# A hybrid encoder layer on one core: all merge gates in the hyena stage, hyena's half of the merge ahead of the last softmax, joint weights spread by transposes

## The chip, the cores and the metric

The kernel runs on one core of a Trainium2 chip. The metric is device time in microseconds of one execution, launch to end; a run's time is given beside the span of its profile, which reaches from the first to the last instruction. A core has TensorE (PE; matmuls and transposes, with its weight loads shown as PEld), VectorE (DVE), ScalarE (ACT), GpSimd (POOL) and SyncE (SP), which issues nearly all of this kernel's DMAs in one queue, in program order.

## The reference

One layer with sequence length 1024 and model width 1024, all in float32. From `h`, a modulated layer norm of `x`, one projection feeds two branches, two silu gates and 2048 merge gates:

```python
h = (_layer_norm(x) * (1.0 + scale) + shift).astype(x.dtype)
p = h @ w_in + b_in
p_qkv, g_attn, p_hy, g_hy, r_merge = jnp.split(p, [i1, i2, i3, i4], axis=-1)
r_attn, r_hy = jnp.split(r_merge, 2, axis=-1)
...
    o_g, lse_g = dilated_window_attention(qkv[:, :, 0, g], qkv[:, :, 1, g], qkv[:, :, 2, g],
                                          slopes, dilation, radius)
...
wts = jax.nn.softmax(jnp.stack(lses, axis=0), axis=0)
o_attn = jnp.einsum('gbsh,gbshe->bshe', wts.astype(x.dtype), jnp.stack(outs, axis=0))
y_attn = o_attn.reshape(B, S, D_ATTN) * jax.nn.silu(g_attn)
...
for o, gate_o in enumerate((x1, x2)):
    z = gate_o * (bidirectional_long_conv(z, filters[:, o, 0], filters[:, o, 1]) + filt_bias[o] * z)
y_hy = z * jax.nn.silu(g_hy)

merged = jax.nn.sigmoid(r_attn) * (y_attn @ w_proj_attn) + jax.nn.sigmoid(r_hy) * (y_hy @ w_proj_hyena)
out = merged @ w_out + b_out
res = DEEPNORM_ALPHA * x.astype(jnp.float32) + (gate * out).astype(jnp.float32)
return (_layer_norm(res) * ln_g + ln_b).astype(x.dtype)
```

There are eight heads of 64 in three groups (window, dilation): (128, 1), (512, 4), (2048, 16). The joint weights `wts` say, per head and position, how much each group's output counts.

## The kernel before

Channels lie on the 128 partitions and positions along the free axis, so a product's output is a tile of 128 channels by 512 positions. Each matrix product is done in three passes: every operand is split into a high and a low part of reduced precision (fp32r), and high x high, high x low and low x high are summed in one PSUM tile. So every weight slice costs a ScalarE cast (`wh`, L222) and a GpSimd subtraction (`wl`, L223), and `h` itself is kept as two resident tiles `hTh` and `hTl` of 128 x 8 x 1024. The function `proj` makes one slice of 128 output channels as two products of 24 matmuls of 512 columns (L242).

The stages in program order:
- norm, filters and hyena (to about 640 us): four long convolutions, each a chain of transforms whose short products (`z`, `q`, `px`) alternate with VectorE and ScalarE work (`f`, `yh`, `yl`). They stand in `conv_order`, at a high priority of the scheduler; other products fill in between them.
- attention (640 to 1258 us), four pairs of heads, some 146 us each: `qkv` projections, the first softmax with one group, `values_pi` for the other two groups' values, `silu_out` (the silu gate of the pair's output), the second softmax with two groups (`softmax_av`, L906 to L934, tiles `ss`, `sx`, `pp`, `pt`, `po`), and the joint weights (L1022 to L1058). The last use of `h` in a pair is `silu_out`.
- merge and output (1258 us to the end): for each half of the positions, eight slices, each with a product of 12 matmuls with the hyena output and one of 12 with the attention output, each multiplied by its gate; their sum is split and goes into the output product with `w_out` (24 matmuls a group, L1138), followed by the residual, the last norm and the stores.

A merge gate is one slice of `proj` with a tanh, stored to `r_d` in DRAM: `gate_r`. There are sixteen, 0 to 7 for attention and 8 to 15 for hyena. `fill(n)` places the next n of the early ones; `N_EARLY` (12) says how many are early, `GATES` and `FILLS` how many stand behind each filter and each convolution. With 12 early, the last entry of `FILLS` finds none left. Gates 12 to 15 stand in a loop after attention:

```python
for j in range(N_EARLY, 16):
    gate_r(j, lambda: at.tile([P, 1152], F32, name="thr", tag="tmp")[:, 0:512])
hctx.close()
```

The joint weights `f` of a pair (2 orders x 8 blocks x 2 heads for 128 positions) have to be spread over the 64 channels of each head. Before, one transpose makes 32 rows of them (`pp` to `fr`, L1039), these go to DRAM (`wt_d`), and four DMA loads bring them back repeated over 64 partitions (`wt`). VectorE multiplies both parts with them, adds, multiplies with the silu gate and stores `ho` to `ya_d` (L1052 to L1058).

The merge loop (L1074 to L1109) loads the halves of `yh_d` and `ya_d` and splits them, then for each slice loads both weights into one tile `wr`, splits it, loads two gates `thr`, and does the two products `pj` (L1103), the gating (L1104), the sum (L1105) and the split into `mh`, `ml` (L1107, L1108). In the first half `w_out` is loaded behind it (L1121), eight tiles of 128 x 1024 through two buffers `wor`, each split by ScalarE (`woh`, L1122) and VectorE (`wol`, L1123).

The order of the instructions is made by a scheduler that walks the program with priorities; memory comes from pools, in which a tile of a tag waits for the release of an older one (`bufs`), and a pool opened where another was closed waits for that one's last readers. Within an engine, and within SyncE's queue, everything runs strictly in the order so made.

## Time and profile before

| | |
|---|---|
| time, median of 3 runs | 1461.62 us (1458.76 to 1461.76) |
| the profiled execution, its time | 1466.4 us |
| its span | 1464.6 us |
| TensorE busy | 1351.3 us, 92% of the span |
| VectorE, ScalarE, GpSimd busy | 65%, 43%, 19% |
| mean granted clock of TensorE | 0.970 |

Times are microseconds unless marked ns. Busy shares are means over the whole span; a window shows the same for a stretch of it, with the granted TensorE clock (1.00 is its full speed) and the share of the DMA engines' time. The chain of waits is followed back from the last instruction, at each step to what released it. In a timeline, what stands in brackets is the idle time before an instruction and what ended it.

### The profile page before, as it was taken

To read this page: it belongs to the slowest core of one execution; us is meant where nothing else is said; L and a number is where in the kernel's file an instruction comes from. 1 tells how busy PE (TensorE), PEld (TensorE's weight loads), DVE (VectorE), ACT (ScalarE), POOL (GpSimd) and SP (SyncE) were. 2 spreads that over 40 slices of the span, in tenths; PEclk is the share of its full clock that TensorE was granted. 3 is DMA by queue.
4 is the path that set the end of the run, shared out by engine and by line. 5 is a ranking of instruction groups with operands and counts; after the bars stand their busy time and mean duration, and the time that the engine had idled before them with its cause. 6 is when DMAs were issued, how large, how long until landed. Compare 5 with 4: busy or idle time off the path is not lost.

```text
span 1464.6 us, 18389 instructions
## 1 busy us (share of the span) xinstructions
PE 1351.3 (92%) x6707; PEld 1098.4 (75%) x6707; DVE 957.6 (65%) x1709; ACT 624.4 (43%) x1220; POOL 282.2 (19%) x160
## 2 busy tenths in 40 slices
PE   4788979889899999999999999999999999689997
PEld 1467767767777777788988788878887888567886
DVE  4798768767999898745156714761466144288866
ACT  1544444534244443446355534663466343242110
POOL 1221121210113122141121112111211111231220
PEclk9799999999999999999999999999999999899999
DMA  9633544332112222121113421311131114588523
GB/s 255 182 97 105 175 133 149 110 130 79 54 58 69 87 65 79 58 84 30 44 59 116 103 61 58 92 30 43 59 91 31 44 58 123 184 249 220 158 88 72
DMA packets 157024, 145.86 MB, mean 100 GB/s; under 512 B 16611, under 2 KB 126591, under 8 KB 156678
## 3 DMA queue, kind: packets, MB, share of 16 engines
q1 hardware_dynamic: 156486, 140.44, 32.7%
q0 software_dynamic: 288, 4.19, 0.8%
q8 instruction: 53, 0.87, 0.3%
q14 instruction: 37, 0.30, 0.1%
q10 hardware_dynamic: 160, 0.06, 0.0%
HBM read 116.73 MB, written 27.92 MB: 99 GB/s over the span
## 4 chain that ended last, share of the span: by engine, by line
PE 64%; DVE 11%; DMA 5%; ACT 3%; issue 2%; POOL 1%; SPq 0%; DVEq 0%; ACTq 0%; POOLq 0%
PE pj L242 33%; PE pj L888 6%; PE z L521 6%; PE po L1138 6%; PE pj L1103 4%; PE po L929 2%; PE pp L922 2%; DVE iv L447 2%; DVE f L447 1%; DMA dk<-in_t_dec 1%; DMA wor<-in_w_out 1%; PE z L531 1%; PE ss L859 1%; DVE f L459 1%; DVE q L447 1%
## 5 line engine op out<-in xcount | busy, mean ns | idle before, releaser
L223 POOL TENSOR_TENSOR wl<-wr,wh 128x1024 fp32r<-128x1024 f32 x88 | 234.8, 2668 | 966.9 <-ACT wh L222 895.7
L242 PE MATMUL pj<-hTh,wh 128*128 128x512 f32 x1024 | 407.5, 398 | 4.0 <-ACT hTh L433 4.0
L242 PE MATMUL pj<-hTl,wh 128*128 128x512 f32 x1024 | 407.1, 398 | 1.5 <-POOL hTl L435 0.8
L242 PE MATMUL pj<-hTh,wl 128*128 128x512 f32 x1024 | 408.1, 399 | 0.0
L242 PEld LDWEIGHTS pj<-hTl,wh 128*128 128x128 f32 x1024 | 194.3, 190 | 40.5 <-DVE hTl L435 2.2
L242 PEld LDWEIGHTS pj<-hTh,wh 128*128 128x128 f32 x1024 | 194.4, 190 | 39.9 <-ACT hTh L433 4.1
L242 PEld LDWEIGHTS pj<-hTh,wl 128*128 128x128 f32 x1024 | 194.4, 190 | 37.3 <-issue 1.0
L222 ACT CAST wh<-wr 128x1024 fp32r<-128x1024 f32 x88 | 92.4, 1050 | 239.5 <-PE pj L242 82.3
L499 ACT CAST yh<-f 128x512 fp32r<-128x512 f32 x88 | 54.1, 615 | 105.2 <-DVE f L447 93.9
L899 DVE TENSOR_TENSOR tmp<-pj,bv 128x512 f32<-128x512 f32 x16 | 11.1, 692 | 115.0 <-PE pj L888 115.0
L500 DVE TENSOR_TENSOR yl<-f,yh 128x512 fp32r<-128x512 f32 x88 | 65.6, 756 | 22.2 <-ACT yh L499 19.9
L521 PE MATMUL z<-yh,tcon 128*128 128x512 f32 x224 | 65.7, 411 | 8.6 <-ACT yh L499 8.6
L918 ACT ACTIVATE sx<-sx,stat 128x256 f32<-128x256 f32 (+1 forms) x128 | 71.6, 563 | 3.1 <-DVE stat L916 3.0
L916 DVE CUSTOM_DVE_ANT_0 sx<-ss,tab 128x384 f32<-128x384 f32 (+1 forms) x112 | 53.7, 492 | 29.2 <-PE ss L844 18.0
L888 PE MATMUL pj<-wh,hTh 128*128 128x256 f32 x256 | 72.7, 284 | 0.0
L888 PE MATMUL pj<-wl,hTh 128*128 128x256 f32 x256 | 72.6, 284 | 0.0
L888 PE MATMUL pj<-wh,hTl 128*128 128x256 f32 x256 | 72.6, 284 | 0.0
L925 DVE TENSOR_TENSOR pt<-pp,pt 128x256 fp32r<-128x256 f32 (+1 forms) x128 | 61.8, 486 | 14.9 <-ACT pt L924 13.6
L1103 PE MATMUL pj<-yh,wl 128*128 128x512 f32 x128 | 52.0, 406 | 17.8 <-ACT yh L1084 11.3
L924 ACT CAST pt<-pp 128x256 fp32r<-128x256 f32 (+1 forms) x128 | 52.2, 425 | 33.4 <-PE po L929 28.9
L922 PE MATMUL pp<-ident,sx 128*128 128x128 f32 x320 | 58.3, 280 | 4.2 <-DVE pt L925 2.7
L521 PEld LDWEIGHTS z<-yh,tcon 128*128 128x128 f32 x224 | 40.6, 191 | 22.3 <-ACT yh L499 15.0
(236 smaller groups left out, 2546.2 us busy)
## 6 DMA issues: line engine op xcount, KB each, us to landing
wr<-in_w_in SPq DMA_DIRECT2D x64, 512.0 KB
xt<-in_x SPq DMA_DIRECT2D x32, 256.0 KB
wa<-in_w_ada SPq DMA_DIRECT2D x16, 512.0 KB
dk<-in_t_dec SPq DMA_DIRECT2D x32, 256.0 KB
r_d<-thr SPq DMA_DIRECT2D x32, 256.0 KB
h_dram<-hs SPq DMA_DIRECT2D x32, 256.0 KB
ht<-h_dram SPq DMA_DIRECT2D x32, 256.0 KB
thr<-r_d SPq DMA_DIRECT2D x32, 256.0 KB
```

Of the source, the lines that this page charges most:

```text
L222: ACT.copy(wh[:, :k, :], src)
L223: PO.tensor_tensor(wl[:, :k, :], src, wh[:, :k, :].bitcast(F32), ALU.subtract)
L242: PE.matmul(ps, w[:, kt, :], h[:, kt, sl], start=i == 0, stop=i == len(ops) - 1)
L447: V.tensor_tensor(o, a, b, op)
L500: V.tensor_tensor(yl[:, c, :], y, yh[:, c, :].bitcast(F32), ALU.subtract)
L521: PE.matmul(z, m, v, start=k == 0, stop=k == 5)
L888: PE.matmul(ps[:, t % 2], h[:, 4 * q + k, P * t : P * t + P], w[:, 2 * k : 2 * k + 2, :], start=first and t % 2 == 0 and i == 0, stop=last ...
L918: ACT.activation(sx[:, : n * P], sx[:, : n * P], AF.Exp, bias=stat[:, t, e, 0:1], scale=-1.0, accum_out=stat[:, t, e, 1:2])
L922: PE.transpose(pp[:, a * P : (a + 1) * P], sx[:, a * P : (a + 1) * P], ident)
L925: V.tensor_tensor(pt[:, :n, 1, :], blk(pp), pt[:, :n, 0, :].bitcast(F32), ALU.subtract)
L1103: PE.matmul(ps, w[:, 4 * b + kt, :], y[:, kt, :], start=i == 0, stop=i == len(ops) - 1)
L1138: PE.matmul(po, m[:, P * q : P * q + P], w[:, kt, ds_], start=n == 0, stop=n == 23)
```

## The change

All sixteen gates become early: `N_EARLY` is 16 and `FILLS` (4, 2, 4, 1), and the loop after attention goes. The pool of `hTh` and `hTl` moves to the other side of the memory and is closed in the last pair after `silu_out`, ahead of its second softmax; a pool `op` opens there for the split attention output of the first half (`y0h`, `y0l`), for `yr` and for the gates.

The joint weights no longer go through DRAM. ScalarE copies `f` broadcast over 64 columns into `fe` (two tiles of 128 x 1024 a pair), TensorE transposes it in sixteen pieces into four PSUM tiles `pw`, and VectorE multiplies with these directly, in eight operations of 512 columns instead of four of 1024. In the last pair, the first half of the output is split at once and not stored.

The merge is divided. A new loop does hyena's part for all eight slices and both halves (`y1`, split from `yh_d`): product, gate, store to `m_d` in DRAM. The merge loop proper does attention's part alone, loads the hyena result `m2` from `m_d`, and adds. The loading of `w_out` and all behind it is as before.

```diff
-N_EARLY = 12
+N_EARLY = 16
-FILLS = (3, 1, 4, 4)
+FILLS = (4, 2, 4, 1)
...
+    hpool = hctx.enter_context(tc.tile_pool(name="hpool", bufs=1, reuse_waits="tile", side="right"))
...
             v23 = values_pi(pr)
             silu_out(pr)
+            if pr == 3:
+
+                hctx.close()
+                op = octx.enter_context(tc.tile_pool(name="op", bufs=2, reuse_waits="tile", side="right"))
+                y0h, y0l = [op.tile([P, 4, 512], F32R, name="y0" + x, tag="y0" + x, bufs=1) for x in "hl"]
...
-            PE.transpose(pp[0:32, 0:P], f.rearrange("p o t e -> p (o t e)"), ident)
...
-            SY.dma_start(wt_d[pr], fr)
...
+            for half in range(2):
+                sl, rs = slice(512 * half, 512 * half + 512), slice(8 * half, 8 * half + 8)
...
+                ACT.copy(fe.rearrange("p o t (e c) -> p o t e c", e=2),
+                         f[:, :, 4 * half : 4 * half + 4, :].unsqueeze(4).to_broadcast([P, 2, 4, 2, HD]))
+                for od in (1, 0):
+                    pw = ps_p.tile([P, 512], F32, name="pw", tag="pp")
+                    for q in range(4):
+                        PE.transpose(pw[:, P * q : P * q + P], fe[:, od, q, :], ident)
+                    if od:
+                        V.tensor_tensor(yb[:, sl], yb[:, sl], pw, ALU.mult)
+                    else:
+                        V.tensor_tensor(yv[:, rs], yv[:, rs], pw.rearrange("p (r t i) -> p r t i", r=8, t=8), ALU.mult)
+                V.tensor_tensor(yw[:, rs], yw[:, rs], yv[:, rs], ALU.add)
+                V.tensor_tensor(yb[:, sl], yb[:, sl], sg[:, sl], ALU.mult)
+                if pr == 3 and half == 0:
+
+                    ACT.copy(y0h[:, 3, :], yb[:, sl])
...
-        for j in range(N_EARLY, 16):
-            gate_r(j, lambda: at.tile([P, 1152], F32, name="thr", tag="tmp")[:, 0:512])
-    hctx.close()
...
+        def split_y(yh_, yl_, src, ks, sl):
+
+            yr = op.tile([P, 2, 512], F32, name="yr", tag="yr")[:, : len(ks), :]
+            SY.dma_start(yr, src[ks.start : ks.stop, :, sl].rearrange("k p s -> p k s"))
+            for i, k in enumerate(ks):
+                ACT.copy(yh_[:, k, :], yr[:, i, :])
+                V.tensor_tensor(yl_[:, k, :], yr[:, i, :], yh_[:, k, :].bitcast(F32), ALU.subtract)
...
+        def merge_product(w, y, sl):
+            ps = ps_w.tile([P, 512], F32, name="pj", tag="mm")
+            ops = [(a, b, kt) for kt in range(4) for a, b in ((w[1], y[0]), (w[0], y[1]), (w[0], y[0]))]
...
+            for sl in (H0, H1):
+                for k in (0, 2):
+                    split_y(y1[0][:, :, sl], y1[1][:, :, sl], yh_d, range(k, k + 2), sl)
+            for k in (range(0, 2), range(2, 3)):
+                split_y(y0h, y0l, ya_d, k, H0)
+            for j in range(8):
+                w = merge_w("w_proj_hyena", j)
+                for sl in (H0, H1):
+                    th = op.tile([P, 512], F32, name="thr", tag="thr", bufs=4)
+                    SY.dma_start(th, r_d[8 + j, :, sl])
+                    ps = merge_product(w, y1, sl)
+                    V.scalar_tensor_tensor(th, th, 1.0, ps, ALU.add, ALU.mult)
+                    SY.dma_start(m_d[j][:, sl], th)
...
             mg = []
             for j in range(8):
...
+                w = merge_w("w_proj_attn", j)
                 m2 = ow.tile([P, 512], F32, name="m2", tag="m2")
...
+                SY.dma_start(m2, m_d[j, :, sl])
+                th = op.tile([P, 512], F32, name="thr", tag="thr", bufs=4)
+                SY.dma_start(th, r_d[j, :, sl])
+                ps = merge_product(w, (y0h, y0l), H0)
+                V.scalar_tensor_tensor(th, th, 1.0, ps, ALU.add, ALU.mult)
+                V.tensor_tensor(m2, m2, th, ALU.add)
```

In the listings below a line is an engine's row in the order of issue, with output, inputs and the output's shape; all lines from L172 on have moved in the changed file.

**ScalarE at the end of the hyena stage.** `yh`, `yl` and `v` belong to the last convolution, `thr` of L252 and `sg` to the silu gate of hyena, `tmp` of L781 to attention's first query. Before:

```order
L638 COPY v<-z 128x512
L222 CAST wh<-wr 128x1024
L252 ACTIVATE thr<-pj,hbias 128x512
L499 CAST yh<-f 128x512
L511 ACTIVATE yh<-f 128x256
L253 ACTIVATE sg<-pj,hbias 128x512
L512 ACTIVATE yl<-yl 128x256
L252 ACTIVATE thr<-pj,hbias 128x512
L222 CAST wh<-wr 128x1024
L252 ACTIVATE thr<-pj,hbias 128x512
L253 ACTIVATE sg<-pj,hbias 128x512 x2
L222 CAST wh<-wr 128x1024
```

Now, where `thr` of L266 is that of a merge gate and L253 and L254 are the silu gate:

```order
L500 CAST yh<-f 128x512
L512 ACTIVATE yh<-f 128x256
L513 ACTIVATE yl<-yl 128x256
L266 ACTIVATE thr<-pj,hbias 128x512
L223 CAST wh<-wr 128x1024
L266 ACTIVATE thr<-pj,hbias 128x512 x2
L223 CAST wh<-wr 128x1024
L266 ACTIVATE thr<-pj,hbias 128x512 x2
L223 CAST wh<-wr 128x1024
L266 ACTIVATE thr<-pj,hbias 128x512
L253 ACTIVATE thr<-pj,hbias 128x512
L254 ACTIVATE sg<-pj,hbias 128x512
```

Behind the last convolution's last `yh` and `yl` there now stand merge gates, then the silu gate that before lay partly beside the convolution.

**SyncE around the loads of `w_out`.** `wr` is a weight slice, `thr` a gate, `m_...` the hyena result. Before:

```order
L1094 DMA wr<-in_w_proj_hyena 128x4x128
L1094 DMA wr<-in_w_proj_attn 128x4x128
L1098 DMA thr<-r_d 128x512
L1121 DMA wor<-in_w_out 128x1024
L1098 DMA thr<-r_d 128x512
L1121 DMA wor<-in_w_out 128x1024
L1094 DMA wr<-in_w_proj_hyena 128x4x128
L1098 DMA thr<-r_d 128x512
L1094 DMA wr<-in_w_proj_attn 128x4x128
L1121 DMA wor<-in_w_out 128x1024
```

Now, with the loads of `m_d` for slices 4 to 7 among them:

```order
L1126 DMA m_11480<-m_d 128x512
L1128 DMA thr<-r_d 128x512
L1080 DMA wr<-in_w_proj_attn 128x4x128
L1128 DMA thr<-r_d 128x512
L1140 DMA rs<-gate_d 128x1024
L1126 DMA m_11509<-m_d 128x512
L1126 DMA m_11538<-m_d 128x512
L1147 DMA wor<-in_w_out 128x1024 x2
L1126 DMA m_11567<-m_d 128x512
L1154 DMA xt<-in_x 64x1024 x2
L1147 DMA wor<-in_w_out 128x1024 x2
```

The loads of `w_out` stand behind those of the hyena result, of which each waits for a buffer that an earlier slice gives back.

**TensorE in the last softmax.** `ss` are the scores, `pp` the transposes, `po` the values' product, `pj` of L242 a product with `h` (a merge gate) and `pj` of L1087 the hyena part of the merge. Before:

```order
L844 MATMUL ss<-kl,q 128x128
L859 MATMUL ss<-ks,qs 128x256
L860 MATMUL ss<-kl,qs 128x256
L844 MATMUL ss<-kl,q 128x128
L242 MATMUL pj<-hTl,wh 128x512
L242 MATMUL pj<-hTh,wl 128x512
L859 MATMUL ss<-ks,qs 128x256
L860 MATMUL ss<-kl,qs 128x256
L844 MATMUL ss<-kl,q 128x128
L929 MATMUL po<-pt,v 128x256 x3
```

Now:

```order
L845 MATMUL ss<-kl,q 128x128
L860 MATMUL ss<-ks,qs 128x256
L861 MATMUL ss<-kl,qs 128x256
L845 MATMUL ss<-kl,q 128x128
L923 MATMUL pp<-ident,sx 128x128 x6
L1087 MATMUL pj<-y1h,wl 128x512
L930 MATMUL po<-pt,v 128x256 x6
L860 MATMUL ss<-ks,qs 128x256
L861 MATMUL ss<-kl,qs 128x256
L845 MATMUL ss<-kl,q 128x128
```

Between the softmax's pieces stand matmuls of the hyena product now where gates stood.

## Rows read from the trace of the kernel before

**Rows 1.** The page's busy time, share of the span and instructions of each engine.

```profile
PE 1351.3 (92%) x6707; PEld 1098.4 (75%) x6707; DVE 957.6 (65%) x1709; ACT 624.4 (43%) x1220; POOL 282.2 (19%) x160
```

**Rows 2.** Windows through the later convolutions and into attention: the stretch and its length, then busy us (and instructions) of PE, PEld, DVE, ACT and POOL, the granted clock, the DMA share and GB/s.

```profile
386.00:468.00 82.00, 77.38 (x334) 61.60 (x334) 72.81 (x135) 35.25 (x68) 16.93 (x4) 0.97 0.17 53
468.00:551.00 83.00, 77.16 (x347) 61.17 (x347) 72.65 (x124) 36.84 (x70) 14.49 (x5) 1.00 0.25 78
551.00:613.00 62.00, 58.93 (x244) 44.93 (x244) 48.62 (x83) 28.40 (x59) 10.44 (x4) 0.97 0.23 73
613.00:640.00 27.00, 27.00 (x126) 21.97 (x127) 19.97 (x40) 5.99 (x9) 9.00 (x3) 1.00 0.28 90
640.00:660.00 20.00, 20.00 (x99) 16.69 (x98) 6.68 (x10) 13.40 (x21) 9.44 (x11) 1.00 0.21 59
```

**Rows 3.** TensorE's timeline in a projection with `h` and in the last softmax: start, duration of one (of all, where xN), instruction.

```profile
1000.48 0.39 PE L242 MATMUL pj<-hTh,wl 128*128 128x512 f32 x1
...
1001.39 0.39 PE L242 MATMUL pj<-hTh,wh 128*128 128x512 f32 x1
...
1198.51 0.27 PE L922 MATMUL pp<-ident,sx 128*128 128x128 f32 x1
1198.98 0.71 PE L922 MATMUL pp<-ident,sx 128*128 128x128 f32 x5
```

**Rows 4.** Windows of the end, columns as in rows 2: the last softmax, gates 12 to 15, the first half of the merge with the loading of `w_out`, the second half's output product, and what follows the last matmul.

```profile
1192.00:1222.50 30.50, 29.85 (x204) 25.08 (x203) 24.73 (x72) 22.34 (x60) 2.39 (x1) 1.00 0.11 35
1222.50:1257.50 35.00, 34.44 (x153) 28.21 (x151) 5.76 (x6) 8.05 (x11) 7.17 (x3) 1.00 0.51 151
1257.50:1329.00 71.50, 53.26 (x213) 42.34 (x213) 47.92 (x51) 24.44 (x32) 20.08 (x8) 0.88 0.76 239
...
1411.70:1455.50 43.80, 43.79 (x216) 37.06 (x214) 29.57 (x54) 0.62 (x1) 2.89 (x3) 1.00 0.26 61
1455.50:1464.60 9.10, 0.00 (x0) 0.00 (x0) 4.34 (x9) 0.00 (x0) 0.92 (x1) 0.73 0.26 58
```

**Rows 5.** The chain of waits through the end: start, duration, engine or DMA, what, and how many instructions in a row.

```profile
1181.32 10.91 PE pj L242 x48
...
1222.68 34.27 PE pj L242 x151
...
1261.27 6.15 DMA yr<-yh_d
...
1318.81 7.22 DMA wor<-in_w_out
...
1329.02 39.07 PE po L1138 x171
1368.09 43.57 PE pj L1103 x192
1411.66 43.84 PE po L1138 x216
```

**Rows 6.** VectorE's timeline around the end of the last softmax: its last remainder, the copy of the transposed joint weights, and the two operations that wait for them.

```profile
1220.58 0.56 DVE L925 TENSOR_TENSOR pt<-pp,pt 128x384 fp32r<-128x384 f32 x1
...
1221.63 0.28 DVE L1039 COPY fr<-pp 32x128 f32<-32x128 f32 x1
...
1230.39 1.23 DVE L1052 TENSOR_TENSOR ho<-ho,wt 128x1024 f32<-128x1024 f32 x1 [6.38 <-DMA wt<-wt_d]
...
1232.44 1.23 DVE L1055 TENSOR_TENSOR ho<-ho,wt 128x1024 f32<-128x1024 f32 x1 [0.82 <-DMA wt<-wt_d]
```

**Rows 7.** Groups of instructions by line in the first merge (1258 to 1329 us): line, engine, operation, count; busy us and mean ns of one; idle time before them and what ended it.

```profile
L1105 DVE TENSOR_TENSOR mt<-mt,m 128x512 f32<-128x512 f32 x8 | 11.3, 1414 | 0.2
L1108 DVE TENSOR_TENSOR ml<-mt,mh 128x512 fp32r<-128x512 f32 x8 | 10.2, 1275 | 3.1 <-ACT mh L1107 3.0
...
L1104 DVE SCALAR_TENSOR_TENSOR mt<-thr,pj 128x512 f32<-128x512 f32 x8 | 5.5, 685 | 2.8 <-PE pj L1103 1.6 <-DMA thr<-r_d 1.1
L1107 ACT CAST mh<-mt 128x512 fp32r<-128x512 f32 x8 | 5.0, 619 | 11.2 <-DVE mt L1105 11.2
L1116 POOL TENSOR_TENSOR bbo<-bbo,rs 128x1024 f32<-128x1024 f32 x1 | 2.9, 2856 | 0.0
```

**Rows 8.** SyncE's queue with the first and the last issue of a `w_out` tile (8 in all) and the one before the last, then ScalarE's cast of that one's tile, then the two groups that split `w_out`.

```profile
1286.74 0.43 SPq L1121 DMA_DIRECT2D wor<-in_w_out  x1
...
1313.29 0.33 SPq L1121 DMA_DIRECT2D wor<-in_w_out  x1
...
1318.81 0.37 SPq L1121 DMA_DIRECT2D wor<-in_w_out  x1
...
1317.01 1.05 ACT L1122 CAST woh<-wor 128x1024 fp32r<-128x1024 f32 x1 [2.37 <-DMA wor<-in_w_out]
...
L1122 ACT CAST woh<-wor 128x1024 fp32r<-128x1024 f32 x8 | 8.4, 1049 | 14.9 <-DMA wor<-in_w_out 14.7
L1123 DVE TENSOR_TENSOR wol<-wor,woh 128x1024 fp32r<-128x1024 f32 x8 | 9.8, 1222 | 5.8 <-ACT woh L1122 5.8
```

**Rows 9.** The page's DMA issues of the merge and the output: what, over the whole run, and the size of one.

```profile
wr<-in_w_proj_hyena SPq DMA_DIRECT2D x16, 256.0 KB
wor<-in_w_out SPq DMA_DIRECT2D x8, 512.0 KB
thr<-r_d SPq DMA_DIRECT2D x32, 256.0 KB
```

## What I predict

> **What bounds the kernel now.** I read the page's busy table first, then the windows by stage, then the chain of waits through the end, then the timelines of TensorE and of SyncE's queue there. TensorE is busy 92% of the span [rows 1]; what decides is how tight it is in each stage. In the hyena stage it is not tight: in the three convolution windows it is busy 77.4 of 82, 77.2 of 83 and 58.9 of 62 us, with VectorE near 88% in the first two [rows 2], because the convolution's chain runs through VectorE and ScalarE. From 613 us on, when the last convolution's transforms are through, it has no gap: 27.0 of 27 and 20.0 of 20 us [rows 2]. There the reader is to see matmuls at a fixed pitch: five starts from 1000.48 to 1001.39, so 0.2275 us each at 512 columns; five transposes take 0.71 us where one takes 0.27, so 0.11 us each [rows 3].
>
> The end has four pieces [rows 4, 5]. The last softmax runs from 1192.2 (the silu gate's last matmul, 1181.32 + 10.91) to the last split of the weights at 1221.1 [rows 6]: 28.9 us. Then 34.3 us of merge gates, nothing else. Then the first half of the merge and the loading of w_out: 1257.5 to 1329, where TensorE works 53 of 71.5 us, at 239 GB/s of DMA traffic. After 1329 it has no gap again: output product, second merge, output product, and 9.1 us behind the last matmul. From the last split to the end of the span: 1464.6 - 1221.1 = 243.5 us.
>
> **The change part by part.** The durations are of the profiled execution: 1466.4 us, span 1464.6. The median shown is 1461.6, 4.8 lower; the sum below is a difference, put on the median.
>
> *Four gates into the hyena stage.* A gate is two products of 24 matmuls; four are 192, x 0.2275 = 43.7 us. Would the idle time of the convolutions take them? The order says no. I counted TensorE's rows: between the last matmul of the last convolution and attention's first projection stand 26 matmuls before and 232 now, and up to there both have the same number; ScalarE's rows show the same. So the convolutions keep as much filler as they had, and the whole 192 (with 14 transposes that only move) lands where TensorE already has no gap [rows 2]. Price +43.7, no cover; down to 30 if the new filler beside the convolutions happens to suit them better (they leave 4.6 + 5.8 + 3.1 = 13.5 us).
>
> *Joint weights by transposes.* One transpose per pair becomes sixteen: for the first three pairs, where TensorE is the bound, 45 x 0.11 = +5.0 us; the last pair's are in the piece below. The copies on ScalarE (two of 1024 columns, about 1.05 us each like the casts of that size [rows 8]) and eight VectorE operations at about 0.69 instead of four at 1.23 and one at 0.28 [rows 6, 7] I cost at nothing: both engines are under TensorE in those windows. Without that cover, 2 us a pair. What goes is the trip through DRAM, for which VectorE stood 6.38 + 0.82 us in the last pair [rows 6]; it stood beside the gates, so nothing is won.
>
> *The last softmax.* Before, 41 gate matmuls stood between its pieces, 9.3 us; now 12 of the hyena product do. TensorE no longer sets its length, the chain does: VectorE's busy time in the window is 24.7 us and ScalarE's 22.3 [rows 4], and four of the new splits of y (0.62 on ScalarE and 0.69 on VectorE each [rows 7]) come on top of either. Bounds: 24.7, and the old 28.9 with four of them behind it, 28.9 + 4 x 0.69 = 31.7; I take 27, nearer to the row of the busier engine, with some start-up: -1.9 us. TensorE stands about a third of it, and that is the price of having little filler.
>
> *From the last split to the end*, 243.5 us before:
> (1) The first two slices of the hyena product with the last pair's weights: 41 matmuls (9.3), 16 transposes (1.8), the last output group (0.7), and waits on y's second half, of which one load stands in SyncE's queue behind a load that waits for the softmax's last matmul: a load of y took 6.15 us at its worst [rows 5]. Ends 11.8 and 20; I take 13.
> (2) Six more slices, 144 matmuls, 32.8 us; every tile now loads a gate and stores its result (256 KB each way), so +2: 34.8.
> (3) The attention half, 96 matmuls, would be 21.8 us. But the output product needs all of w_out. In SyncE's order the first load of w_out stands behind the load of the hyena result for slice 6, which waits for the split of slice 4, and the second behind a GpSimd multiplication (2.86 us [rows 7]) that waits for all eight splits of the attention weights. Slice 4's product ends 5 x 2.73 = 13.7 us after the first begins, the four operations behind it (evacuation, addition, cast, remainder) take 0.69 + 1.41 + 0.62 + 1.28 = 4.0 at the means of that window or 0.69 x 3 + 0.62 = 2.7 without the slow ones [rows 7]; I take 2.9: first load at 16.6. GpSimd is through at about 21.5. Then a pair of buffers turns over as in the kernel before: eight issues from 1286.74 to 1318.81, 4.6 us apart [rows 8], 1.05 for the cast, 1.22 for the remainder [rows 8], 0.3 for signals, so 7.2 for two. Third load at 24.2; the fifth at 32.3, since four splits of the next half's y (2.7) stand before the third remainder in VectorE's order; the seventh at 39.5, the eighth at 41.5, its remainder ready at 41.5 + 4.6 + 2.6 = 48.7. The first output group ends there, 48.9, where products alone would give 21.8 + 5.4 = 27.2: a new stall of 21.7 us. With landings of 3.7 us (the shortest I saw, the issue at 1313.29 to the cast's start at 1317.01 [rows 8]) it is 44; at the kernel before's pace of 4.6 us for every load, 58.
> (4) The other 168 output matmuls: 38.2.
> (5) The second half's attention product: 21.8 + 2. Per slice VectorE has three operations, 2.1 us at 0.69 each or 0.69 + 1.41 + 1.28 = 3.4 at the means of that window [rows 7], against 2.73 on TensorE. Ends 16.4 (no less than TensorE's 21.8) and 27.6.
> (6) The last output half 43.8 and the end 9.1 [rows 4, 5]: 52.9.
> Sum 13 + 34.8 + 48.9 + 38.2 + 23.8 + 52.9 = 211.6, so -31.9.
>
> A row bears on (5): an addition of two SBUF tiles took 1.41 us in that window, while the evacuation of the same size, with one operand in PSUM, took 0.69 [rows 7]. The Trainium skill (SBUF — State Buffer, Who interferes with whom) says that a VectorE instruction with two SBUF inputs and a GpSimd instruction that reads SBUF exclude each other for a whole instruction. The trace agrees (1.41 against 0.69). By that rule each slice's two SBUF operations wait for at most one weight split of half the old length, an estimate near 3.3 us a slice and 4 to 5 for this half in place of 2.
>
> **Sum.** +43.7 + 5.0 - 1.9 - 31.9 = +14.9 on 1461.6: **1476.5 us**, 1.0% slower. In one sentence: TensorE's work only grows (60 transposes), the gates go from a place without gaps to another without gaps, and the stall in front of the output product stays, since the loads of w_out moved up with the work that hid them.
>
> **The rivals.**
> *w_out is there in time.* Its tiles lie in memory that the softmax gives back, so the loads could run beside the hyena product; if they did, (3) would be 27.2 and the two allowances of 2 would go: -25.7, so 1450.8, faster. For it: TensorE would have over 50 us of cover. Against it: SyncE issues in order, and the order puts these loads where I counted them. 0.18.
> *The convolutions swallow the gates.* If VectorE's pauses there fall where the new filler stands, the 13.5 us of idle TensorE [rows 2] come back: +1.4, 1463.0, no change. Against it: the number of matmuls beside the convolutions is the same. 0.12.
> *DMA is the bound.* From the last split to the last piece of w_out the kernel moves 63 transfers of 256 KB (16 stores and 10 loads of the hyena result, 22 gate tiles, 15 weight slices) and 19 of 512 KB (w_out, four rows spread, y, the silu gate, x) [rows 9]: 26.5 MB. At the 239 GB/s of the first merge [rows 4] that is 111 us against the 96.7 of (1) to (3): +14, so 1490.7. For it: that window was the busiest of the end already. Against it: its DMA share was 0.76, not 1. 0.18.
> On this the Trainium skill (DMA: Bandwidth & Descriptors, Bandwidth) gives about 358 GB/s as a core's share of the memory. No row here reaches it: the busiest window of the end has 239 GB/s. By that rule 26.5 MB would take an estimate of 74 us and could not bind, which speaks for the two rivals above and against this one.
> *The change doesn't do what it says:* the hyena product starts only after the softmax, because y's loads wait for the release of h. Then 12 matmuls move behind it, +3 us; it lies inside the forecast's own range.
>
> **How the numbers follow.** The forecast's case has 0.52. Its own range is 1462 to 1486: 5 less for the shortest landings and 9 less for a good part of the convolutions' idle time, 9 more for the pace of 4.6 us a load. The rivals have 0.18, 0.12 and 0.18. The range that should hold 8 in 10 reaches from 1450, so that it takes in the first rival's own time, to 1491, the third's. About 0.2% (2.9 us) is what a measurement can tell from no change: under 1458.7 lies the first rival and a little of the second, 0.22; between 1458.7 and 1464.5 most of the second and the forecast's lower edge, 0.12; above, 0.66.
>
> **What would show it.** Right: attention's first projection starts about 44 us later than before while the convolutions keep their length; pair to pair the pitch grows by about 1.7 us; from the silu gate's end to the last split about 27 us with TensorE well under full; the hyena product in one block of 40 to 50 us; and a gap of some 20 us before the output product, ended by the remainder or the cast of w_out. Wrong: no such gap (first rival); attention starting less than 35 us later (second); gaps between the hyena slices that end on gate tiles or weight slices, with DMA share near 0.9 (third). A forecast of slower fails altogether if the end from the last split is under 195 us.

## The result

The changed kernel takes 1481.28 us, median of 4 runs (1480.21 to 1482.82), against 1461.47 us before (also 4 runs): a ratio of 1.0141, 95% interval 1.0123 to 1.0158. I forecast 1476.5 (1450 to 1491) and slower with a chance of 0.66. The profiled execution took 1482.0 us with a span of 1480.1, beside 1466.4 and 1464.6 before: 15.5 us more span, which the stretches below account for. The medians lie 19.8 us apart; the profiled execution of the kernel before was 4.9 us above its median, that of the kernel after 0.7.

The page's busy line of the kernel after answers to [rows 1]:

```profile
PE 1360.2 (92%) x6767; PEld 1094.5 (74%) x6767; DVE 942.7 (64%) x1721; ACT 632.7 (43%) x1236; POOL 286.4 (19%) x168
```

TensorE has 60 instructions more (the transposes) and 9 us more of busy time; the share is the same. So the time has not gone into one engine's work but into how it is laid out, and that is read from stretches. I cut the profiled runs at the same marks: start of the last matmul of the last convolution (where I say below that the convolutions end, I mean this mark), first scores of the first and of the last softmax with one group in hand, last split of the softmax weights, 192nd matmul of the output product, last matmul. In us:

| run | last convolution to first scores | to the last softmax | last softmax | to the 192nd output matmul | to the last matmul | tail |
|---|---|---|---|---|---|---|
| before | 43.6 | 535.0 | 29.1 | 146.9 | 87.4 | 9.1 |
| after | 86.7 | 537.0 | 26.8 | 135.7 | 69.2 | 9.2 |

After minus before is +43.1, +2.0, -2.3 and, from the last split on, -29.3 (243.5 to 214.2); the convolutions end 1.8 later (613.5 to 615.3). The forecast had +43.7, +5.0, -1.9 and -31.9.

Windows of the kernel after, columns as in [rows 2]; the first two answer to the last two there, the others to [rows 4]:

```profile
615.30:660.00 44.70, 44.70 (x201) 36.77 (x201) 15.26 (x26) 10.45 (x14) 13.93 (x4) 1.00 0.23 73
660.00:702.00 42.00, 42.00 (x189) 34.56 (x188) 13.52 (x20) 16.16 (x21) 13.50 (x13) 1.00 0.28 86
...
1239.00:1269.00 30.00, 25.21 (x175) 21.07 (x175) 26.13 (x75) 25.24 (x66) 1.28 (x1) 1.00 0.33 108
1269.00:1282.00 13.00, 11.27 (x56) 8.50 (x55) 12.22 (x22) 6.56 (x10) 3.25 (x2) 1.00 0.53 177
1282.00:1320.00 38.00, 37.22 (x163) 30.23 (x163) 8.95 (x14) 4.35 (x7) 8.63 (x8) 1.00 0.91 289
1320.00:1348.00 28.00, 20.98 (x76) 15.59 (x74) 16.07 (x18) 6.00 (x10) 11.54 (x7) 0.82 0.77 245
1348.00:1368.80 20.80, 15.49 (x54) 10.51 (x54) 15.52 (x20) 10.06 (x14) 0.04 (x1) 0.92 0.83 229
```

The reader is to see three things. Behind the last convolution TensorE is busy in every microsecond, so four more gates there cost what they take. In the last softmax it is busy 25.2 of 30 us where before it was 29.9 of 30.5 [rows 4]: the stage is hardly shorter, only emptier. And from 1320 to 1369 it stands still again, 12.3 of 48.8 us, while the DMA share is 0.77 and 0.83 in the two windows.

What it waits for is in the chain of waits of the kernel after (start, duration, what):

```profile
1304.20 6.47 DMA m_d<-thr
1311.58 5.36 DMA m_d<-thr
1317.37 3.78 DMA m_d<-thr
1321.74 6.86 DMA wr<-in_w_proj_attn
1329.40 1.28 POOL wl L224
...
1350.00 3.86 DMA m<-m_d
1354.56 1.23 DVE wol L1149
1355.81 4.72 DMA wor<-in_w_out
1360.55 1.05 ACT woh L1148
1361.63 1.24 DVE wol L1149
1362.88 4.82 DMA wor<-in_w_out
```

[rows 5] show a part of the chain before. Between the load of y and the last load of w_out it also held

```profile
1282.04 5.34 DMA thr<-r_d
...
1288.56 6.45 DMA wor<-in_w_out
...
1308.91 4.66 DMA wor<-in_w_out
```

so one load of y, one gate and three tiles of w_out in all. Now it runs through a row of stores of the hyena result, weight slices, a load of that result and two tiles of w_out.

### The profile page after: what moved, and what is told of

Same layout as the page of the kernel before. It is cut to its first block, busy times and chain, and to the rows that moved or that the text cites. A ratio compares the mean times of both kernels' runs of the same rounds, so it can differ in the third digit from the quotient of the medians.

```text
span 1480.1 us, 18592 instructions
## 1 busy us (share of the span) xinstructions
PE 1360.2 (92%) x6767; PEld 1094.5 (74%) x6767; DVE 942.7 (64%) x1721; ACT 632.7 (43%) x1236; POOL 286.4 (19%) x168
## 4 chain that ended last, share of the span: by engine, by line
PE 56%; DVE 13%; DMA 7%; ACT 4%; issue 2%; POOL 1%; SPq 0%; DVEq 0%; ACTq 0%; POOLq 0%
PE pj L243 30%; PE pj L889 6%; PE z L522 5%; PE po L1164 5%; PE pp L923 2%; PE po L930 2%; DMA m_d<-thr 2%; DVE f L448 2%; DVE iv L448 2%; DVE y L609 1%; PE ss L860 1%; DMA wr<-in_w_proj_attn 1%; ACT pt L925 1%; ACT sx L919 1%; DVE q L448 1%
## 5 line engine op out<-in xcount | busy, mean ns | idle before, releaser
L224 POOL TENSOR_TENSOR wl<-wr,wh 128x1024 fp32r<-128x1024 f32 (+1 forms) x96 | 232.3, 2420 | 908.4 <-ACT wh L223 811.3
L223 ACT CAST wh<-wr 128x1024 fp32r<-128x1024 f32 (+1 forms) x96 | 90.5, 943 | 285.5 <-issue 106.8
L501 DVE TENSOR_TENSOR yl<-f,yh 128x512 fp32r<-128x512 f32 x88 | 62.0, 713 | 20.9 <-ACT yh L500 17.8
L930 PE MATMUL po<-pt,v 128*128 128x256 f32 x320 | 55.6, 294 | 2.0 <-DVE ho L935 1.8
```

The costliest lines, as they stand in the source:

```text
L223: ACT.copy(wh[:, :k, :], src)
L224: PO.tensor_tensor(wl[:, :k, :], src, wh[:, :k, :].bitcast(F32), ALU.subtract)
L501: V.tensor_tensor(yl[:, c, :], y, yh[:, c, :].bitcast(F32), ALU.subtract)
L930: PE.matmul(po[:, t % 2], v[:, 2 * e : 2 * e + 2, :], pt[:, a], start=a == 0, stop=a == n - 1)
```

## The experiments

All runs were compared with runs of the kernel before on the same chip (medians 1462.93, 1461.99 and 1461.67 us in the three sets). Single runs scattered more than in the result, by some 0.6% to either side. Part of that lies ahead of everything the parts touch: the last convolution ends at 613.5 us in the profile of before and at 606.4 in that of the joint weights alone, whose code is the same up to there. So I read profiles from that mark on.

### Which part costs what

*The gates alone*, on the kernel before:

```diff
-N_EARLY = 12
+N_EARLY = 16
-FILLS = (3, 1, 4, 4)
+FILLS = (4, 2, 4, 1)
```

> The kernel before with one edit: all sixteen gates in the hyena stage, nothing else. My theory (TensorE has no free time behind the last convolution, so a gate costs its full 10.9 us there): +43.7 us up to attention, -34.3 us for the block of 151 matmuls behind the last softmax, the softmax itself 0 to 3 us shorter without filler, and 0 to 8 us more because nothing covers the DRAM trip of the last pair's joint weights any more: 1466 to 1479 us. Rival (the convolutions swallow part of the gates): attention starts less than 35 us later, 1452 to 1465 us.

Measured: 1494.57 us, ratio 1.0213 (1.0174 to 1.0252), the slowest kernel of all. The first stretch is 86.0 us, +42.4: the gates cost their full price there, and the convolutions swallowed nothing. From that mark on the profile holds 20.2 us more than before, where the medians are 31.6 apart; its convolutions end 6.6 us later. In the nine profiles with the new `FILLS` they end at 610.9 to 620.1 us, in the five with the old one at 606.4 to 613.5. So a few microseconds there may belong to the moved gates too; these runs cannot tell them from scatter.

The end shrank by only 20 us instead of 34. Its chain behind the last softmax:

```profile
1268.95 1.62 PE po L929 x6
1271.13 3.10 DMA wt_d<-fr
1275.60 1.03 SPq L1049
1276.67 8.26 DMA wt<-wt_d
1285.03 1.24 DVE ho L1055
1286.29 1.23 DVE ho L1057
1287.54 1.24 DVE ho L1058
1289.17 5.11 DMA yr<-yh_d
1295.12 7.92 PE pj L1103 x24
```

and the window that holds it:

```profile
1271.00:1295.00 24.00, 0.00 (x0) 0.00 (x0) 5.85 (x7) 0.64 (x2) 0.00 (x0) 0.50 0.75 202
```

TensorE does nothing for 24 us. This is the trip of the last pair's joint weights through DRAM and their use, which the gates had covered, and the load of y, which they had not: before, TensorE stood 11.3 us between the last gate and the merge.

```profile
1268.26 0.77 PE L1103 MATMUL pj<-yh,wl 128*128 128x512 f32 x1 [11.32 <-ACT yh L1084]
```

I had allowed 0 to 8 us for the uncovered trip; it was 13 (24.3 less 11.3).

*The joint weights alone*, on the kernel before: the code with `fe` and `pw` in all four pairs, with both halves stored.

> The kernel before with the joint weights spread by transposes, nothing else. My theory (only TensorE's added transposes count, the DRAM trip was hidden in every pair): 3 x 15 x 0.11 = +5.0 us in the first three pairs and up to +1.8 us in the last, 1465 to 1469 us. Rival (the DRAM trip held something up in the first pairs, so its removal pays for the transposes): 1461.5 us or less.

Measured: 1468.17 us, 1.0041 (1.0018 to 1.0064). From the first to the last softmax 539.1 us, +4.1 for 45 transposes where I had 5.0. The rival is out: in the kernel before that trip held up no more than the 0.9 us between these two.

*Both together*, with the merge as before:

> The kernel before with all sixteen gates in the hyena stage and the joint weights spread by transposes; the merge as before. The run with the gates alone showed TensorE idle for 24.3 us behind the last softmax, in which the joint weights' trip through DRAM lies. Theory A (once the gates are gone, that trip is on the path, and the transposes take it off): the gap shrinks to 10 to 15 us, and with +5 us for the transposes of the first pairs the time is 1484 to 1492 us, under the 1494.6 of the gates alone. Theory B (the gap is made by the store and the loads of y, not by the weights' trip): the gap stays over 20 us and the time is 1496 to 1502 us.

Measured: 1481.95 us, 1.0132 (1.0088 to 1.0176). Theory A's gap is there, and the time is 2 us under its range; theory B is out. The same stretch of the chain is now

```profile
1271.24 1.10 PE pw L1048 x4
1277.14 7.02 DMA yr<-yh_d
1284.99 19.37 PE pj L1099 x72
```

and the gap 11.6 us (1273.44 to 1284.99). So the transposes, which cost 5 us by themselves, pay once the gates are gone. How much is less sure than the medians say, which are 12.6 us apart. From the last split on the profile is 10.0 us shorter than with the gates alone (213.2 against 223.1), and the transposes of the first pairs cost 4.1, so 5.9 net. The two profiles differ by another 5.8 us ahead of the mark, where TensorE's instructions are the same in both.

And this kernel, which has no early hyena part of the merge, is as fast as the full change (1.0132 against 1.0141, intervals that overlap). The largest edit of the three is worth nothing that these runs can tell: it fills the gap in front of the merge, and as much comes back behind it. TensorE's time from the last split to its last matmul is 116.7 + 87.3 = 204.0 us here and 135.7 + 69.2 = 204.9 in the full change.

### Where the end of the full change loses its time

*w_out loaded earlier.* The loads move from behind the first attention half into the loop of the hyena product:

```diff
+            load_wo(j)
...
-                for kt in range(KT):
-                    wr = ow.tile([P, D], F32, name="wor", tag="wor")
-                    SY.dma_start(wr, wo[P * kt : P * kt + P, :])
```

> The changed kernel with one edit: the loads of w_out stand in the loop of the hyena product, one per slice, instead of behind the first attention half. My theory (the output product waits because SyncE's order issues w_out late): the waits on w_out in front of and inside the first output groups go, 10 to 18 us of TensorE's lost time, 1463 to 1471 us. DMA rival (the hyena product's window already moves 289 GB/s at a share of 0.91, so 4.2 MB more there only push other loads back by up to 14 us): 1476 to 1484 us, with gaps inside the hyena and attention products.

Measured: 1480.54 us, 1.0132 (1.0097 to 1.0168): no gain, and inside the DMA rival's range, with gaps inside the hyena product as it said. This is the run that speaks against my step (3). From the last split to the 192nd output matmul it is 134.4 us, where the full change has 135.7. TensorE's own waits there, with idle time and releaser in brackets:

```profile
1291.60 0.47 PE L1101 MATMUL pj<-y1h,wl 128*128 128x512 f32 x1 [2.98 <-DVE thr L1119]
...
1309.93 0.79 PE L1101 MATMUL pj<-y1h,wl 128*128 128x512 f32 x1 [5.49 <-POOL wl L224]
```

w_out is there, and gates and weight slices are late instead; the window from 1278 to 1316 has a DMA share of 0.91 at 303 GB/s.

*More buffers, three ways.* Six buffers for the returning hyena result on top of the early w_out; four buffers of their own for the attention weights on the changed kernel; and, on top of the early w_out, four buffers for the result and a tile of its own for each gated product from slice 2 on:

```diff
+                m2 = ow.tile([P, 512], F32, name="m2", tag="m2", bufs=6)
```
```diff
+                raw = ow.tile([P, 4, P], F32, name="wa", tag="wa", bufs=4)
```
```diff
+                mo = th if j < 2 else mp.tile([P, 512], F32, name="mo", tag="mo")
+                V.scalar_tensor_tensor(mo, th, 1.0, ps, ALU.add, ALU.mult)
```

> The changed kernel with w_out loaded in the hyena loop and six buffers instead of two for the hyena result on its way back (the same DMAs, issued earlier). Buffer theory (each slice of the attention part waits for a load of 4 to 7 us that is issued only when one of two buffers is free): the waits in front of the output product and in the second half go, 1469 to 1475 us. Volume theory (the DMA engines are the bound there, so the same bytes take the same time): 1477 to 1482 us.

> The changed kernel with four buffers of their own for the attention weights of the merge instead of two shared ones. Theory A (the 6.5 us in which TensorE waits before the fourth attention slice come from a weight slice that could only be loaded when a buffer was free, since each slice is now used for one product and not two): that wait goes, but the output product then waits for w_out, 1475 to 1481 us. Rival (the load itself is slow under the DMA traffic): the wait stays within 2 us, 1479 to 1483 us.

> The changed kernel with w_out loaded in the hyena loop, four buffers for the hyena result on its way back, and from slice 2 on the gated product in a tile of its own, so that a gate's buffer is free again as soon as it is multiplied and not only when the store is through. The same bytes in nearly the same order. Buffer theory (gates and weight slices come late because a buffer turns over only after a load, a product and a store): 1462 to 1472 us. Volume theory (the DMA engines are busy at 0.83 to 0.98 from the first hyena slices to the output product, so the same bytes take the same time): 1476 to 1483 us.

Measured: 1481.89 (1.0135, 1.0089 to 1.0182), 1482.00 (1.0142, 1.0108 to 1.0176) and 1482.77 us (1.0129, 1.0083 to 1.0175). None gains. With four weight buffers the wait in front of the fourth attention slice did not vanish but stood in front of the first one:

```profile
1324.28 0.80 PE L1087 MATMUL pj<-y0h,wl 128*128 128x512 f32 x1 [9.99 <-POOL wl L224]
```

So none of these buffers is the limit by itself. No run loosens all of them at once.

*Fewer bytes, two ways.* First, five of the eight hyena results of the first half stay on the chip, on top of the early w_out:

```diff
+                if sl is H0 and j >= 3:
+                    m0[j] = mp.tile([P, 512], F32, name="m0", tag=f"m0{j}")
+                    V.scalar_tensor_tensor(m0[j], th, 1.0, ps, ALU.add, ALU.mult)
+                    continue
```

> The changed kernel with w_out loaded in the hyena loop and, of the first half, the hyena result of slices 3 to 7 kept on the chip instead of being stored and loaded again: 10 transfers of 256 KB fewer. With the early loads alone nothing was gained (1480.5). Volume theory (from the softmax to the output product the end is bound by what the DMA engines move, 280 to 300 GB/s at a share of 0.9): 2.6 MB less are 9 us, 1468 to 1474 us. Rival (what binds is SyncE's order and the waits for weight slices and gates): 1476 to 1482 us.

Measured: 1477.93 us, 1.0110 (1.0079 to 1.0142), inside the rival's range, not the volume theory's, and not clear of the 1.0132 of the early w_out alone (the intervals overlap). Second, on the run with loosened buffers, one gate tile is loaded and all slices are multiplied with it; the other 31 gate loads are left out:

```diff
-                SY.dma_start(th, r_d[8 + j, :, sl])
...
-                SY.dma_start(th, r_d[j, :, sl])
```

> The run before it with one thing less: the merge gates are not loaded back, one gate tile serves all slices of both parts, so 31 loads of 256 KB (8.1 MB) are left out; the order of stores and of all other loads in SyncE's queue stays. Volume theory: the 23 of them that lie ahead of the output product are 6.0 MB, at 290 GB/s 20 us; of TensorE's some 27 us without work there at least 12 come back, 1462 to 1468 us. Queue theory (SyncE issues in order, and each store of a hyena result holds the loads behind it until its product is done): 1474 to 1480 us.

Measured: 1471.53 us, 1.0071 (1.0040 to 1.0102): 11.2 us under the run it was made from, between the two ranges. The stretch to the 192nd output matmul falls from 134.6 to 125.8. The 60 us from 1286 to 1346, first with the gates loaded, then without:

```profile
1286.00:1346.00 60.00, 49.71 (x197) 39.50 (x196) 29.07 (x34) 17.09 (x23) 15.41 (x10) 0.89 0.88 285
```
```profile
1286.00:1346.00 60.00, 53.53 (x221) 42.05 (x220) 33.55 (x38) 18.23 (x25) 20.76 (x13) 0.97 0.86 275
```

With 6 MB fewer to move ahead of the output product the DMA engines are as busy as before, and TensorE gets 24 matmuls further. Of all edits to the full change this alone gained clear of noise, which points to traffic. It does not single out the bytes, though: the same edit takes 31 issues out of SyncE's queue and frees the products from waiting for a gate. And bytes alone do not set the time, or the first run would have gained the 9 us worked out for it. SyncE's own waits in these 60 us (what it waited for, us in total, times, longest), the first two lines with the gates loaded, the others without:

```profile
SPq L1122 <- DVE mo L1121: 19.5, 11, 5.6
SPq L1095 <- POOL wl L224: 6.6, 5, 2.0
...
SPq L1122 <- DVE mo L1121: 15.5, 7, 4.0
SPq L1095 <- POOL wl L224: 9.1, 4, 5.1
```

L1122 is the store of a hyena result, L1095 the load of a weight slice. Together SyncE stands 26.1 of 60 us for the product that it must store next and for a weight buffer, with the later loads behind it, and 24.6 when the gates go. Whether this queue, the bytes, or the cost of the small rows of a weight slice makes the rest of the loss stays open.

### A way that beats both

The 11.3 us before the merge in the kernel before come from memory: the split y lies where h was, so its loads wait for the last gate. Three kernels keep gates 12 to 15 behind the last softmax, put h on the other side of the memory and use attention's freed tiles beside those gates.

*w_out beside the gates:*

> The kernel before with one edit of another kind: gates 12 to 15 stay behind the last softmax, but attention's memory is given back ahead of them and w_out is loaded and split beside them. My theory (what the end loses is the wait on w_out, 18 us of TensorE in the first merge): 1443 to 1450 us. Rival (the loads of y, gates and weight slices bind that merge anyway): 1456 to 1462 us.

Measured: 1472.19 us, 1.0082 (1.0051 to 1.0112), slower; the loads of y still come late, and TensorE stands 12.7 us in front of the merge. *y beside the gates:*

> The kernel before with gates 12 to 15 still behind the last softmax, but h on the other side of the memory, so that the split y of the first half and the buffers of w_out lie where attention's tiles were; y is loaded and split beside those gates. Theory (TensorE stands 11.3 us between the last gate and the first merge product because y's tiles wait for h): that gap falls to 0 to 2 us, and the time is 1447 to 1454 us. Rival (the loads only move, and the merge then waits for gates, weights and w_out as much longer): 1458 to 1464 us.

Measured: 1462.84 us, 1.0003 (0.9976 to 1.0031), no change. Neither came near my theory. In the second the gates run into the merge without a gap, as expected, but both kernels have a new wait that I had put there myself. ScalarE in the second of them, at the first gate's evacuation:

```profile
1237.98 1.26 ACT L265 ACTIVATE thr<-pj,hbias 128x512 f32<-128x512 f32 x2 [14.79 <-DMA ya_d<-ho]
```

and TensorE, in the row of its gate matmuls:

```profile
1238.72 0.80 PE L242 MATMUL pj<-hTh,wh 128*128 128x512 f32 x1 [10.93 <-ACT thr L265]
```

The gates' result tile had come to lie on attention's memory, so the first gate could not be evacuated until the last pair's output was stored, and TensorE stood 10.9 us for that evacuation. What delays that store is the joint weights' trip, so in the third kernel the last pair alone uses the transposes:

```diff
+            if pr == 3:
+                for half in range(2):
...
+            else:
+                pp = ps_p.tile([P, 512], F32, name="pp", tag="pp")
```

> The same as the run before it, and the joint weights spread by transposes in the last pair alone, where the trip through DRAM delays the store of y, and not in the first three, where the transposes cost TensorE 1.4 us a pair. Theory: +1.8 us of transposes, and the loads of y come some 8 us earlier, so no gate waits for ScalarE: 1446 to 1454 us. Rival (beside the gates that trip costs nothing): 1 to 3 us over the run before it.

Measured: 1454.65 us, 0.9954 (0.9929 to 0.9979): faster than the kernel before by 0.5%, 27 us under the changed one, and 0.7 us above the range I gave. The same wait is half as long,

```profile
1230.74 1.27 ACT L265 ACTIVATE thr<-pj,hbias 128x512 f32<-128x512 f32 x2 [7.39 <-DMA ya_d<-ho]
```

TensorE stands 3.5 us there, and the gates run straight into the merge (the last gate matmul ends at 1261.28, the first of the merge starts at 1261.12).

```profile
1231.48 0.50 PE L242 MATMUL pj<-hTh,wh 128*128 128x512 f32 x1 [3.53 <-ACT thr L265]
```

Not all of the gain is explained by this. The medians are 7.0 us under the kernel before, the profile from the last split on 3.3 (240.2 against 243.5). And of the 7.4 us that TensorE stands less than in the second kernel 6.1 reach the output product and 3.2 are left after its first half; the last section shows why. Put elsewhere, that tile would give some of the 3.5 us back; this was not tried.

## Why the prediction was right, point by point

**The gates.** Right, and in size: +43.1 where +43.7 was said, in a place where TensorE has no gap. The run with the gates alone shows nearly the same, +42.4. The second rival, that the convolutions swallow them, is out.

**Joint weights.** The price of the transposes was 5.0; alone they cost 4.1, in the full change 2.0, a difference that I did not follow up. "Nothing is won" by dropping the trip was true of the kernel before only: it was hidden by the gates that the same change takes away. Without them its removal is worth 5.9 us net by the profiles, 12.6 by the medians. The sum of the forecast did not need this, since TensorE waits for that trip in neither the kernel before nor the one after.

**The last softmax.** Right in size, -2.3 for -1.9. TensorE was to stand a third of it; it stands 4.2 of the 26.8 us, a sixth.

**From the last split to the end.** -29.3 where -31.9 was said; by its terms:

| term | forecast | measured |
|---|---|---|
| (1) two hyena slices with the last transposes | 13 | 15.1 |
| (2) six hyena slices | 34.8 | 34.1 |
| (3), (4) attention half, first output half | 87.1 | 85.4 |
| (5), (6) second half and end | 76.7 | 79.6 |

Measured are the last split (1265.9), the starts of the third hyena slice (1281.0) and of the attention half (1315.1), the end of the 192nd output matmul (1401.6) and the end (1480.1), with 1.1 us for five matmuls of the second half, which run early, moved from the third line to the fourth. The fourth line was put 2.9 too low: in the second half TensorE waits 1.5 and 1.6 us for splits of weight slices.

**Step (3) failed in its mechanism.** It said that the loads of w_out come late because of their place in SyncE's queue, and that the first output group stalls 21.7 us for the eighth. Their place was as counted: the first pair is issued behind the load of the hyena result for slice 6, and pairs follow at 8.2, 8.8 and 5.7 us.

```profile
1344.09 4.31 SPq L1147 DMA_DIRECT2D wor<-in_w_out  x2
...
1352.34 3.80 SPq L1147 DMA_DIRECT2D wor<-in_w_out  x2
...
1361.09 2.12 SPq L1147 DMA_DIRECT2D wor<-in_w_out  x2
...
1366.74 3.64 SPq L1147 DMA_DIRECT2D wor<-in_w_out  x2
```

Counted from the start of the attention half, all is later than forecast, by 12 us at the first load and at the last remainder (1375.9, not 1363.8), because TensorE first lost 6.5 us in front of the fourth attention slice and because loads were slow. In exchange the output product did not wait for the eighth tile: the order has four output groups advance together as w_out comes in, and 72 of the 192 matmuls, those with the first six tiles, were through by 1373, with waits of 2.3, 0.5, 1.3 and 1.1 us. So the gap of some 20 us that was to show the forecast right was not there. TensorE lost 11.0 us inside the attention half (32.8 us for 96 matmuls, 21.8 at the usual pitch) and 8.8 us in the output product behind it, 19.8 in all where the one stall was put at 21.7. Two errors of about a dozen microseconds cancelled; that the sum of (3) and (4) came out within 2 us is luck. And the run with the early loads shows that w_out's place was not the cause at all: with it mended, nothing is gained. That is the first rival with its condition met, and it takes 1480.5, not 1450.8. In w_out's place TensorE waits there for gated products, weight slices and the split sums.

**The third rival was nearer to the cause than I gave it credit for.** It said that 26.5 MB at 239 GB/s take 111 us from the last split to the last piece of w_out. The window from 1265.9 to 1376.0 has 252 GB/s over 110.1 us, 27.7 MB. Its duration was right; its price of +14 was not, since the output product went on meanwhile. Its premise of one fixed rate was not either, since 38 us of it moved 289 GB/s. I had weighed it down with the 358 GB/s that the Trainium skill (DMA: Bandwidth & Descriptors, Bandwidth) gives as a core's share. The runs here show why that was no argument: at 289 GB/s the engines' time was already taken to 0.91. Ten microseconds of the kernel after (1287 to 1297) moved 297 GB/s at a share of 0.99, ten of the kernel before (1263 to 1273) 354 at 0.99. So what full engines move depends on the transfers, and it is the share that tells how full they are.

**Two SBUF operands beside GpSimd.** The estimate that I drew from the Trainium skill (SBUF — State Buffer, Who interferes with whom) was 3.3 us of VectorE a slice in the second half. The rows of 1400 to 1433 us give 0.67 + 0.93 + 0.77 = 2.4, of which the addition and the remainder are the two with both operands in SBUF:

```profile
L1131 DVE TENSOR_TENSOR m<-m,thr 128x512 f32<-128x512 f32 x8 | 7.5, 932 | 1.0 <-DMA m<-m_d 0.9
L1134 DVE TENSOR_TENSOR ml<-m,mh 128x512 fp32r<-128x512 f32 x8 | 6.2, 771 | 3.5 <-ACT mh L1133 3.4
```

They are shorter than the 1414 and 1275 ns of [rows 7], beside weight splits that are half as long. The direction agrees with the rule, and the waits were fewer than one a slice.

## What to carry to other kernels

Work that fills a tight place has a second value, the latencies that it hides; before moving it, list what runs beside it (here a trip through DRAM, 13 us) and price that too. Judge a bundle of edits by its parts: here the gates cost 2.1%, the joint weights took back 0.8% (half of it seen in the profiles) that was only there to take because of the gates, and the large rewrite of the merge was worth nothing measurable. When a single wait is mended and the next one grows by the same amount, as in four runs here, look at what all the late things share before mending the next.

## What the runs showed that I had not expected

A wait can cost more than its length, because the granted clock falls in it. After the 6.5 us in front of the fourth attention slice the next 13 matmuls ran at a granted clock of 0.50, the 1.2 GHz level, and took 5.5 us:

```profile
1324.20:1330.70 6.50, 0.00 (x0) 0.00 (x0) 4.01 (x6) 2.33 (x4) 1.27 (x1) 0.67 0.93 315
1330.70:1336.20 5.50, 5.48 (x13) 4.32 (x14) 2.82 (x3) 0.66 (x2) 1.54 (x1) 0.50 0.80 249
```

At the pitch of 0.2275 us [rows 3] they would take 3.0, so the wait cost 9.0 us in place of 6.5.

It does not always do so. In front of the output product TensorE waits 2.84 us in the kernel with y beside the gates and 2.90 in the one with the transposes in its last pair. The next 6 us of the one, then of the other:

```profile
1327.10:1333.10 6.00, 5.93 (x26) 4.93 (x27) 4.29 (x9) 2.29 (x5) 2.21 (x1) 1.00 1.01 301
1319.10:1325.10 6.00, 5.96 (x14) 4.71 (x15) 4.37 (x8) 2.86 (x5) 2.45 (x1) 0.50 0.84 266
```

After nearly the same wait one keeps its clock, with 26 matmuls, and the other has the 1.2 GHz level, with 14. That is the 2.8 us more that the first output half takes in the faster kernel (41.9 against 39.1).
